# A decoder layer with 32 experts: nine named homes for the expert weights, filled in the order they come free

## The chip, the cores and the metric

The kernel runs on one core of one Trainium2 chip. The metric is the device time of one execution in microseconds (us), the median of several. Engines are named as in the profile: PE is TensorE's matmuls, PEld its weight loads, DVE is VectorE, ACT is ScalarE, POOL is GpSimd, and SP is the engine whose queue issues nearly all transfers here (the profile calls its issuing part SPq).

## The reference

One decoder layer on 256 rows of width 1024, float32. Two attention branches and an output projection come first. Then each row goes to 4 of 32 experts, and each expert has an up-projection to 2 x 1024 columns, a clamped gate, and a down-projection. The part of it that the change touches:

```
h = layer_norm(DN_ALPHA * x + mix @ w_out, ln1_g, ln1_b)
logits = h @ w_router + b_router
top_vals, top_idx = lax.top_k(logits, 4)
gates = jax.nn.softmax(top_vals)
combine = jnp.sum(jax.nn.one_hot(top_idx, 32) * gates[..., None], axis=1)
def expert(acc, p):
    wu, bu, wd, bd, c = p
    a = t @ wu + bu                                  # wu: 1024 x 2048
    g = jnp.minimum(a[:, :1024], 7.0)
    lin = jnp.clip(a[:, 1024:], -7.0, 7.0)
    y = ((lin + 1.0) * (g * jax.nn.sigmoid(1.702 * g))) @ wd + bd   # wd: 1024 x 1024
    return acc + c[:, None] * y, None
x = layer_norm(DN_ALPHA * h + ffn, ln2_g, ln2_b)
```

## The kernel before

**Two stages.** The first stage is attention and its projections. Its weights (`w_pre`) come in 1 MB tiles and are split into a high and a low part for products in three passes: ScalarE copies the high part (L149), VectorE subtracts it (L150). The pieces have names such as `wh`, `sh`, `sy`, `sacc`. This stage ends with the routing. The second stage runs the experts in 16 pairs, each expert with room for 64 rows, both experts of a pair side by side on TensorE. Rows are gathered by products with 0/1 tables (`pm`, L786), up-products are L1032, down-products L1039, and the result is scattered back to rows (L997) and added to `acc`. A check of the rows per expert (`nblk_i`) can start a loop for experts with more rows than that; with these inputs it isn't needed.

**Weights of the experts.** An expert has 8 MB of up-weights and 4 MB of down-weights. They are loaded in blocks of 2.097 MB (128 partitions x 4096 float32): `fetch_up(e, k, t)` (L961), k = 0 to 3, and `fetch_down(e, a, t)` (L965), a = 0 or 1. A pair therefore takes 12 blocks. There is room for nine blocks, 16 KB per partition each: three pools `ring4` (1), `ring3` (5) and `ringx` (3). They lie where buffers of the first stage lay, so the first block in each can be issued only when the first stage no longer reads that space. Below, the nine places are called as the changed kernel calls them: right3 is `ring4`, left0 to left4 are the five of `ring3`, right0 to right2 the three of `ringx`. `slot2()` hands them out round and round, in the order that `rings` sets:

```
rings((ring4, 1), (ring3, 3), (ringx, NX2), (ring3, NL2 - 3))
```

that is right3, left0, left1, left2, right0, right1, right2, left3, left4. The 10th block takes right3 again, and so on.

**Four halves.** For experts 0 and 1 the block k = 3 comes in halves of 1 MB, into places that are still free then: `one2`, the space of `acc` (before `acc` is used), `one1`, and `wy` in the space of `y`. They are issued by L976.

**Order.** PE, DVE and ACT issue in source order in the pair loop (`tc.manual_schedule`). SP isn't in that list: its order comes from the framework's scheduler, which may move a transfer ahead of others or behind them. SP's queue is served in order, so a transfer that waits for its space holds up all that stand behind it.

**Biases of the up-projection.** `b_up` comes in four groups of three pieces (`braw`, L575). POOL converts each to `bup` (L581, L586). `next_bup` is called before the pair loop for the first group and in the loop, at experts 2, 10 and 18, for the others.

**The last four experts** are written out behind the loop; their last down blocks come in a half (L1098) and three smaller pieces (L1103), expert by expert.

Of the kernel before, what the change touches and what calls it, by code (L numbers as in the profile page):

```python
# [10 lines left out]
F32 = mybir.dt.float32  # L11
F32R = mybir.dt.float32r
BF16 = mybir.dt.bfloat16
EN = mybir.EngineType
# [6 lines left out]
P = 128  # L21
# [3 lines left out]
KD = D // P  # L25
# [3 lines left out]
NE, TOPK, FF = 32, 4, 1024  # L29
CAP = 64  # L30
NR1, NR2, NSP = 7, 5, 3
NL2, NX2 = 5, 3
ALPHA = 2.0 ** 0.25
LN_EPS, RMS_EPS = 1e-5, 1e-6
LIMIT, SW = 7.0, 1.702
# [23 lines left out]
def decoder_layer(ctx: ExitStack, tc: tile.TileContext, A, dbg=None):  # L59
    nc = tc.nc  # L60
    te, ve, se, ge, sy = nc.tensor, nc.vector, nc.scalar, nc.gpsimd, nc.sync
# [26 lines left out]
    def slot2():  # L88

        turn[0] += 1  # L90
        return seq[(turn[0] - 1) % len(seq)].tile([P, 4096], F32, name="w2")

    def rings(*pools):
        turn[0] = 0
        seq[:] = [p for p, n in pools for _ in range(n)]
# [7 lines left out]
    src = tc.alloc_tile_pool(name="src", bufs=1)  # L103
# [36 lines left out]
    def part(w, a, k, to=None):  # L140

        if spare:
            hi, lo = spare[flip[0] % len(spare) if to is None else to]
        else:
            hi, lo = [att.tile([P, 1024], F32R, name=n, bufs=NSP) for n in ("wh", "wl")]
        n = w.shape[2]
        hi, lo = hi[:, :n], lo[:, :n]
        flip[0] += 1
        se.copy(hi, w[:, a])  # L149
        (ge if flip[0] in aside else ve).tensor_sub(lo, w[:, a], hi.bitcast(F32))  # L150
        return [t.rearrange("p (k c) -> p k c", k=k) for t in (hi, lo)]
# [396 lines left out]
    moe = ctx.enter_context(tc.tile_pool(name="moe", bufs=1, reuse_waits="tile", side="right"))  # L548
# [99 lines left out]
    for j in range(KD):  # L648
# [3 lines left out]
        w = part(wo, j % 2, KD)  # L652
# [4 lines left out]
        t = held["g", j][1]  # L657
        ve.tensor_mul(t, ps, t)
        ve.tensor_add(t[:, 0], t[:, 0], t[:, 1])
        if j:  # L660
            w = part(wu, (j - 1) % 2, 1)
# [15 lines left out]
    w = part(wu, 1, 1)  # L677
# [215 lines left out]
    acc = per.tile([P, NT, D], F32, name="acc")  # L893
# [1 line left out]
    ring1.release()  # L895
    xrows.release()
    ring2.release()
    ring3 = ctx.enter_context(tc.tile_pool(name="ring3", bufs=NL2, reuse_waits="tile"))
    one1 = ctx.enter_context(tc.tile_pool(name="one1", bufs=1, reuse_waits="tile"))
    ringx = ctx.enter_context(tc.tile_pool(name="ringx", bufs=NX2, reuse_waits="tile", side="right"))  # L900
    one2 = ctx.enter_context(tc.tile_pool(name="one2", bufs=1, reuse_waits="tile", side="right"))
    ring4 = ctx.enter_context(tc.tile_pool(name="ring4", bufs=1, reuse_waits="tile", side="right"))
    rings((ring4, 1), (ring3, 3), (ringx, NX2), (ring3, NL2 - 3))

    def add_rows(b, c, ps):
        ve.tensor_add(acc[:, b, half(c)], acc[:, b, half(c)], ps)  # L906
# [23 lines left out]
    def up_view(e):  # L930
        return A["w_up"][e].rearrange("(k p i) f -> p k (i f)", p=P, i=2)
# [25 lines left out]
    def halves_of(t):  # L957
        return t[:, :2048], t[:, 2048:]
# [5 lines left out]
    def fetch_down(e, a, t):  # L964
# [1 line left out]
        return halves_of(t)  # L966


    ahead = [(fetch_up, i, k) for k in range(KD // 2) for i in range(2)][:-2]
    ahead += [(fetch_down, i, a) for a in range(2) for i in range(2)][:NL2 + NX2 + 1 - len(ahead)]  # L970
    early = {(f, e, k): f(e, k, slot2()) for f, e, k in ahead}
    late = [[one2.tile([P, 2048], F32, name="w"), acc.rearrange("p b d -> p (b d)")],
            [one1.tile([P, 2048], F32, name="w"), moe.tile([P, 2048], F32, name="wy", tag="y")]]
    for i in range(2):
        for t, src in zip(late[i], halves_of(up_view(i)[:, KD // 2 - 1])):
            sy.dma_start(t, src)  # L976
        early[fetch_up, i, KD // 2 - 1] = late[i]

    def fetch(f, e, k):
        return early.pop((f, e, k)) if (f, e, k) in early else f(e, k, slot2())  # L980
# [7 lines left out]
    def parts_of(dn, gs):  # L988
        y = moe.tile([P, 2, FF], F32R, name="yp", tag="y")
        for c in range(2):  # L990
            parts(y, dn, gs, c)
        return y
# [33 lines left out]
    with order:  # L1026
# [18 lines left out]
        for ea in range(0, NE - 4, 2):  # L1045
# [16 lines left out]
            y = moe.tile([P, 2, FF], F32, name="y")  # L1062
# [19 lines left out]
            y = parts_of(dn, gs)  # L1082
# [34 lines left out]
        y = moe.tile([P, 2, FF], F32, name="y")  # L1117
# [39 lines left out]
        y = parts_of(dn, slots_a[1])  # L1157
# [130 lines left out]
    with tc.If(most > 1):  # L1288
        at = slot2()[:, :2048].rearrange("p (v n) -> p v n", v=4)
# [106 lines left out]
```

## Time and profile before

| what | value |
|---|---|
| median of 3 runs (lowest to highest) | 1192.05 us (1191.5 to 1192.13) |
| the profiled execution: its own time | 1190.18 us |
| its span in the profile | 1188.5 us |
| busy: PE, PEld, DVE, ACT, POOL | 93%, 47%, 28%, 19%, 11% |
| bytes moved | 439.71 MB, mean 370 GB/s over the span |
| chain that ended last, by engine | DMA 43%, PE 41%, DVE 2%, ACT 1% |

The span is what the rows below divide up. Busy shares are means over stages: the first stage moves few bytes and the second many, so the table of the profile in 40 slices and the views of single stages tell more than the means. In rows with a bracket, the number in it is the idle time just before, and behind the arrow stands what ended it.

### The profile page before, as it was taken

To read this page: it belongs to the slowest core of one execution; us is meant where nothing else is said; L and a number is where in the kernel's file an instruction comes from. 1 tells how busy PE (TensorE), PEld (TensorE's weight loads), DVE (VectorE), ACT (ScalarE), POOL (GpSimd) and SP (SyncE) were. 2 spreads that over 40 slices of the span, in tenths; PEclk is the share of its full clock that TensorE was granted. 3 is DMA by queue.
4 is the path that set the end of the run, shared out by engine and by line. 5 is a ranking of instruction groups with operands and counts; after the bars stand their busy time and mean duration, and the time that the engine had idled before them with its cause. 6 is when DMAs were issued, how large, how long until landed. Compare 5 with 4: busy or idle time off the path is not lost.

```text
span 1188.5 us, 13798 instructions
## 1 busy us (share of the span) xinstructions
PE 1109.3 (93%) x5807; PEld 554.2 (47%) x5808; DVE 332.6 (28%) x698; ACT 221.7 (19%) x427; POOL 135.9 (11%) x127
## 2 busy tenths in 40 slices
PE   8999999979999999999999999999999999999985
PEld 8987889724343443333333343333333433334322
DVE  7887637603111221111111111111111111112013
ACT  4567634311010110001010101010101010101011
POOL 6573673000000100000001000000000000000001
PEclk9999999989999999999999999999999999999998
DMA  8433752599999999999999999999999999999991
GB/s 323 178 108 142 264 189 84 228 426 427 427 427 428 426 416 427 428 426 429 425 429 426 427 428 427 426 427 427 427 428 426 428 426 427 428 426 428 427 410 69
DMA packets 37740, 439.71 MB, mean 370 GB/s; under 512 B 5621, under 2 KB 5866, under 8 KB 9386
## 3 DMA queue, kind: packets, MB, share of 16 engines
q1 hardware_dynamic: 37674, 438.79, 88.4%
q8 instruction: 47, 0.77, 0.3%
q14 instruction: 19, 0.16, 0.0%
HBM read 437.72 MB, written 1.05 MB: 369 GB/s over the span
## 4 chain that ended last, share of the span: by engine, by line
DMA 43%; PE 41%; DVE 2%; ACT 1%; issue 0%; SPq 0%; DVEq 0%; ACTq 0%
DMA w<-w_up 37%; PE bank L1039 15%; PE pair L1032 13%; DMA w<-w_down 5%; PE misc L786 4%; PE misc L926 1%; PE pair L1039 1%; ACT y L927 1%; PE misc L158 1%; PE misc L160 1%; PE misc L159 1%; PE pair L159 1%; PE pair L160 1%; PE pair L158 1%; PE misc L997 1%; DMA braw<-b_down 0%
## 5 line engine op out<-in xcount | busy, mean ns | idle before, releaser
L1032 PE MATMUL pair<-w,xg 128*64 128x512 f32 x2032 | 501.1, 599 | 41.8 <-DMA w<-w_up 41.8
L1032 PEld LDWEIGHTS pair<-w,xg 128*64 128x64 f32 x2032 | 150.3, 137 | 352.0 <-issue 272.0
L1039 PE MATMUL bank<-w,y 128*64 128x512 f32 x960 | 218.7, 596 | 5.1 <-DMA w<-w_down 3.4
L1039 PEld LDWEIGHTS bank<-w,y 128*64 128x64 f32 x960 | 73.1, 137 | 132.3 <-issue 109.2
L906 DVE TENSOR_TENSOR acc<-acc,misc 128x512 f32<-128x512 f32 x56 | 36.2, 684 | 173.5 <-PE misc L997 173.3
L158 PE MATMUL bank<-xh,wh 128*128 128x256 f32 x256 | 74.1, 290 | 4.3 <-DVE rm L211 2.5
L1009 ACT CAST pgT<-bank 128x256 fp32r<-128x256 f32 x16 | 6.0, 373 | 374.6 <-PE bank L1007 374.6
L160 PE MATMUL bank<-xh,wl 128*128 128x256 f32 x256 | 73.2, 286 | 2.0 <-DVE wl L150 2.0
L159 PE MATMUL bank<-xl,wh 128*128 128x256 f32 x256 | 72.4, 283 | 0.0
L786 PEld LDWEIGHTS misc<-pm,h 128*128 128x128 f32 x512 | 62.9, 197 | 14.2 <-issue 11.7
L786 PE MATMUL misc<-pm,h 128*128 128x128 f32 x512 | 67.4, 285 | 0.7 <-ACT y L927 0.7
L916 DVE TENSOR_SCALAR y<-pair 128x512 f32<-128x512 f32 x30 | 20.6, 688 | 166.5 <-ACT y L909 166.5
L184 POOL TENSOR_TENSOR rstd<-rstd,mhalf 128x1 f32<-128x1 f32 x4 | 2.3, 571 | 557.7 <-DVE rstd L690 557.7
L985 DVE SCALAR_TENSOR_TENSOR yp<-bank,gsl,yp 128x512 fp32r<-128x512 f32 x30 | 21.1, 747 | 157.8 <-ACT yp L984 157.8
L984 ACT ACTIVATE yp<-bank,gsl 128x512 fp32r<-128x512 f32 x30 | 19.0, 684 | 178.5 <-PE bank L1039 178.5
L158 PEld LDWEIGHTS bank<-xh,wh 128*128 128x128 f32 x256 | 48.8, 191 | 6.4 <-issue 2.6
L149 ACT CAST wh<-w 128x1024 fp32r<-128x1024 f32 (+1 forms) x42 | 42.7, 1024 | 42.6 <-PE bank L159 29.1
L160 PEld LDWEIGHTS bank<-xh,wl 128*128 128x128 f32 x256 | 48.8, 191 | 3.1 <-DVE wl L150 2.9
L159 PEld LDWEIGHTS bank<-xl,wh 128*128 128x128 f32 x256 | 48.9, 191 | 0.2 <-DVE xl L155 0.2
L774 DVE TENSOR_SCALAR xg<-misc,lnx 128x128 f32<-128x128 f32 x64 | 22.1, 404 | 92.5 <-PE misc L786 85.5
L909 ACT ACTIVATE y<-pair 128x512 f32<-128x512 f32 x30 | 17.8, 597 | 158.6 <-PE pair L1032 158.6
L581 POOL CAST bup<-braw 96x512 bf16<-96x512 f32 x4 | 2.4, 607 | 375.5 <-PE pair L800 375.4
(361 smaller groups left out, 1091.5 us busy)
## 6 DMA issues: line engine op xcount, KB each, us to landing
w<-w_up SPq DMA_DIRECT2D x126, 2048.0 KB, 32.8
w<-w_down SPq DMA_DIRECT2D x62, 2048.0 KB, 32.1
w<-w_pre SPq DMA_DIRECT2D x27, 1024.0 KB, 5.1
w<-w_up SPq DMA_DIRECT2D x2, 1024.0 KB, 17.7
w<-w_down SPq DMA_DIRECT2D x2, 1024.0 KB, 29.1
w<-w_pre SPq DMA_DIRECT2D x3, 512.0 KB, 6.7
w<-w_pre SPq DMA_DIRECT2D x2, 768.0 KB, 12.6
w<-xT SPq DMA_DIRECT2D x4, 256.0 KB, 5.7
```

The costliest lines, as they stand in the source:

```text
L149: se.copy(hi, w[:, a])
L158: te.matmul(out, lhs[0], rhs[0], start=start, stop=False)
L159: te.matmul(out, lhs[0], rhs[1], start=False, stop=False)
L160: te.matmul(out, lhs[1], rhs[0], start=False, stop=stop)
L774: ve.tensor_scalar(dst, src, lnx[:, k:k + 1], lnx[:, 8 + k:9 + k], op0=OP.mult, op1=OP.add)
L786: te.matmul(pt[:, k4], columns(b, k), pm[:, b].rearrange("p e s -> p (e s)"), start=(b == 0), stop=(b == NT - 1))
L906: ve.tensor_add(acc[:, b, half(c)], acc[:, b, half(c)], ps)
L916: ve.tensor_scalar(li, up[c][:, 1], LIMIT + 1.0, 1.0 - LIMIT, op0=OP.min, op1=OP.max)
L984: se.activation(y[:, 0, half(c)], dn[c], AF.Copy, scale=gs)
L985: ve.scalar_tensor_tensor(y[:, 1, half(c)], dn[c], gs, y[:, 0, half(c)].bitcast(F32), op0=OP.mult, op1=OP.subtract)
L1032: te.matmul(up[c % 2][64 * i:64 * i + 64, c // 2], xg[k // 4][:, k % 4, 64 * i:64 * i + 64], ws[i][:, 512 * c:512 * c + 512], start=False, ...
L1039: te.matmul(dn[c][64 * i:64 * i + 64, :], aT[:, 2 * a + j, 64 * i:64 * i + 64], ws[i][:, D * j + 512 * c:D * j + 512 * c + 512], start=Fal ...
```

## The change

The three rings become nine pools of one buffer each with names, at the same places. The order in which they are filled is set by a list. The halves of block 3 are issued between the full blocks, behind the 2nd, 6th, 7th and 8th of them (n counts from 0). And from the first expert block on SP issues in source order as well.

```diff
-    ring3 = ctx.enter_context(tc.tile_pool(name="ring3", bufs=NL2, reuse_waits="tile"))
-    one1 = ctx.enter_context(tc.tile_pool(name="one1", bufs=1, reuse_waits="tile"))
-    ringx = ctx.enter_context(tc.tile_pool(name="ringx", bufs=NX2, reuse_waits="tile", side="right"))
-    one2 = ctx.enter_context(tc.tile_pool(name="one2", bufs=1, reuse_waits="tile", side="right"))
-    ring4 = ctx.enter_context(tc.tile_pool(name="ring4", bufs=1, reuse_waits="tile", side="right"))
-    rings((ring4, 1), (ring3, 3), (ringx, NX2), (ring3, NL2 - 3))
+    def home(name, side):
+        return ctx.enter_context(tc.tile_pool(name=name, bufs=1, reuse_waits="tile", side=side))
+
+    left = [home(f"left{i}", "left") for i in range(5)]
+    one1 = home("one1", "left")
+    right = [home(f"right{i}", "right") for i in range(3)]
+    one2 = home("one2", "right")
+    right.append(home("right3", "right"))
+
+    homes = [right[3], right[1], left[1], left[2], left[0], left[3], left[4], right[2], right[0]]
+    rings(*((p, 1) for p in homes))
...
-    ahead = [(fetch_up, i, k) for k in range(KD // 2) for i in range(2)][:-2]
-    ahead += [(fetch_down, i, a) for a in range(2) for i in range(2)][:NL2 + NX2 + 1 - len(ahead)]
-    early = {(f, e, k): f(e, k, slot2()) for f, e, k in ahead}
-    late = [[one2.tile([P, 2048], F32, name="w"), acc.rearrange("p b d -> p (b d)")],
-            [one1.tile([P, 2048], F32, name="w"), moe.tile([P, 2048], F32, name="wy", tag="y")]]
-    for i in range(2):
-        for t, src in zip(late[i], halves_of(up_view(i)[:, KD // 2 - 1])):
-            sy.dma_start(t, src)
-        early[fetch_up, i, KD // 2 - 1] = late[i]
+    early = {}
+    parts_at = [[one2.tile([P, 2048], F32, name="w"), acc.rearrange("p b d -> p (b d)")],
+                [one1.tile([P, 2048], F32, name="w"), moe.tile([P, 2048], F32, name="wy", tag="y")]]
+
+    def fetch_half(e, i):
+        sy.dma_start(parts_at[e][i], halves_of(up_view(e)[:, KD // 2 - 1])[i])
+
+    in_order = ctx.enter_context(tc.manual_schedule(engines={EN.SP}))
+    for n, (f, e, k) in enumerate([(fetch_up, i, k) for k in range(KD // 2 - 1) for i in range(2)]
+                                  + [(fetch_down, 0, 0), (fetch_down, 1, 0), (fetch_down, 0, 1)]):
+        early[f, e, k] = f(e, k, slot2())
+        for at, h_e, h_i in ((1, 0, 0), (5, 0, 1), (6, 1, 0), (7, 1, 1)):
+            if n == at:
+                fetch_half(h_e, h_i)
+    for e in range(2):
+        early[fetch_up, e, KD // 2 - 1] = parts_at[e]
```

Lines of the changed kernel: L961 becomes L965, L965 becomes L969, L976 becomes L979, L575 becomes L574, L1098 and L1103 become L1110 and L1115.

**Where the stages meet, SP.** In the kernel before, from the last two tiles of the first stage (`w<-w_pre`) to the last up blocks of the first pair. Numbered names are full blocks; `w<-w_up 128x2048` and `acc` are halves.

```order
L130 DMA w<-w_pre 128x2048 x2
L961 DMA w_2703<-w_up 128x4096
L575 DMA braw<-b_up 32x512 x6
L976 DMA acc<-w_up 128x2048
L961 DMA w_2705<-w_up 128x4096
L961 DMA w_2707<-w_up 128x4096
L961 DMA w_2709<-w_up 128x4096
L965 DMA w_2717<-w_down 128x4096
L965 DMA w_2719<-w_down 128x4096
L976 DMA w<-w_up 128x2048
L961 DMA w_2711<-w_up 128x4096
L961 DMA w_2713<-w_up 128x4096
```

The first full block is followed by two groups of `b_up` and then by the half in `acc`'s space; the half in `one2` stands earlier, between tiles of the first stage. In the changed kernel the same place on SP reads:

```order
L129 DMA w<-w_pre 128x2048 x2
L965 DMA w_2726<-w_up 128x4096
L965 DMA w_2728<-w_up 128x4096
L979 DMA w<-w_up 128x2048
L965 DMA w_2731<-w_up 128x4096
L965 DMA w_2733<-w_up 128x4096
L965 DMA w_2735<-w_up 128x4096
L965 DMA w_2737<-w_up 128x4096
L979 DMA acc<-w_up 128x2048
L969 DMA w_2740<-w_down 128x4096
L979 DMA w<-w_up 128x2048
L969 DMA w_2743<-w_down 128x4096
```

Six full blocks and the half in `one2` now stand ahead of `acc`'s half, and no `b_up` group is left here.

**In the second pair, SP of the changed kernel.** The rows go from the pair's third up blocks to its first down blocks and show one of the two groups of `b_up` that stood at the place above.

```order
L965 DMA w_3046<-w_up 128x4096
L965 DMA w_3048<-w_up 128x4096
L965 DMA w_3076<-w_up 128x4096
L965 DMA w_3078<-w_up 128x4096
L574 DMA braw<-b_up 32x512 x3
L969 DMA w_3143<-w_down 128x4096
L969 DMA w_3145<-w_down 128x4096
```

The group now stands behind the pair's last up block; the next two stand at the same place of the sixth and the tenth pair. Before, only the last of these three stood among the blocks of the pair loop.

**The end, SP of the changed kernel.** The last down blocks of experts 30 and 31 (`w_5916`, `w_5918`) and the output.

```order
L1110 DMA w_5916<-w_down 128x2048
L1110 DMA w_5918<-w_down 128x2048
L1115 DMA w_5916<-w_down 128x2x512
L1115 DMA w_5918<-w_down 128x2x512
L1115 DMA w_5916<-w_down 128x512
L1115 DMA w_5918<-w_down 128x512
L1115 DMA w_5916<-w_down 128x512
L1115 DMA w_5918<-w_down 128x512
L1214 DMA out<-w_6311 128x512 x4
L1292 TENSOR_LOAD nblk_i
```

Before, all pieces of the one expert stood ahead of those of the other, and SP's read of `nblk_i` stood among the blocks of the second pair. PE, DVE and ACT have the same order as before.

## Rows read from the trace of the kernel before

**Rows 1.** The page, chain that ended last: shares of the span by line.
```profile
DMA w<-w_up 37%; PE bank L1039 15%; PE pair L1032 13%; DMA w<-w_down 5%; PE misc L786 4%; PE misc L926 1%; PE pair L1039 1%; ACT y L927 1%; PE misc L158 1%; PE misc L160 1%; PE misc L159 1%; PE pair L159 1%; PE pair L160 1%; PE pair L158 1%; PE misc L997 1%; DMA braw<-b_down 0%
```
**Rows 2.** Table by stretch: start:end us, busy (count) per engine, PE clock, DMA share, GB/s.
```profile
181.00:189.00 8.00, 8.00 (x66) 7.82 (x65) 6.08 (x9) 4.21 (x6) 0.00 (x0) 1.00 0.80 287
189.00:220.00 31.00, 31.00 (x200) 28.05 (x199) 22.99 (x27) 13.29 (x16) 10.23 (x8) 1.00 0.03 7
260.00:265.00 5.00, 2.12 (x5) 0.53 (x6) 0.00 (x0) 0.00 (x0) 0.00 (x0) 0.50 1.01 429
300.00:428.00 128.00, 127.75 (x645) 50.86 (x641) 24.43 (x48) 12.10 (x24) 4.74 (x6) 1.00 1.01 427
428.00:1080.00 652.00, 617.60 (x2844) 244.98 (x2845) 109.26 (x220) 59.91 (x122) 6.32 (x7) 1.00 1.01 427
```
**Rows 3.** Timeline of ACT, 370 to 430 us: start, duration, instruction; once per pair.
```profile
376.64 0.37 ACT L1009 CAST pgT<-bank 128x256 fp32r<-128x256 f32 x1 [19.95 <-PE bank L1007]
...
428.38 0.37 ACT L1009 CAST pgT<-bank 128x256 fp32r<-128x256 f32 x1 [19.93 <-PE bank L1007]
```
**Rows 4.** The chain in order of time, from 1100 us on: start, duration, what.
```profile
1122.41 32.55 DMA w<-w_down
...
1155.01 3.65 PE pair L1039 x14
```
**Rows 5.** Timeline of SP's queue, 180 to 221 us: start, stretch, what it issues.
```profile
180.99 0.33 SPq L961 DMA_DIRECT2D w<-w_up  x1
181.49 18.31 SPq L575 DMA_DIRECT2D braw<-b_up  x6
220.38 0.35 SPq L976 DMA_DIRECT2D acc<-w_up  x1
```
**Rows 6.** Waits of SP's queue, 181 to 221 us: total us, times, longest.
```profile
SPq L976 <- DVE sacc L150: 14.5, 1, 14.5
...
SPq L575 <- POOL bup L586: 9.0, 1, 9.0
...
SPq L976 <- PE misc L160: 6.0, 1, 6.0
```
**Rows 7.** Timeline of SP's queue, 295 to 296 us.
```profile
295.70 0.33 SPq L961 DMA_DIRECT2D w<-w_up  x1
```
**Rows 8.** DMA issues of the same instant: count, KB each, us to landing.
```profile
w<-w_up SPq DMA_DIRECT2D x1, 2048.0 KB, 9.6
```
**Rows 9.** Timeline of DVE, 165 to 215 us: splits of weights.
```profile
172.97 2.18 DVE L150 TENSOR_TENSOR sy<-w,sy 128x1024 fp32r<-128x1024 f32 x1 [7.02 <-ACT sy L149]
...
184.93 1.22 DVE L150 TENSOR_TENSOR sy<-w,sy 128x1024 fp32r<-128x1024 f32 x1
...
192.96 1.50 DVE L150 TENSOR_TENSOR sh<-w,sh 128x1024 fp32r<-128x1024 f32 x1
...
200.59 1.22 DVE L150 TENSOR_TENSOR sh<-w,sh 128x1024 fp32r<-128x1024 f32 x1
...
210.24 1.22 DVE L150 TENSOR_TENSOR sy<-w,sy 128x1024 fp32r<-128x1024 f32 x1
```
**Rows 10.** DMA issues, 180.5 to 181.4 us: count, KB each, us to landing.
```profile
w<-w_up SPq DMA_DIRECT2D x1, 2048.0 KB, 8.1
```
**Rows 11.** Timeline of PE, 234 to 304 us: products of the first pair.
```profile
236.52 7.09 PE L1032 MATMUL pair<-w,xg 128*64 128x512 f32 x32
...
245.62 7.09 PE L1032 MATMUL pair<-w,xg 128*64 128x512 f32 x32
...
263.41 5.25 PE L1032 MATMUL pair<-w,xg 128*64 128x512 f32 x14 [2.88 <-DMA w<-w_up]
...
284.03 3.65 PE L1039 MATMUL bank<-w,y 128*64 128x512 f32 x16
...
292.02 10.52 PE L1039 MATMUL bank<-w,y 128*64 128x512 f32 x48
```
**Rows 12.** Table by stretch for line L150 alone: busy (count) of DVE, then POOL.
```profile
181.00:236.50 55.50, 18.56 (x14) 0.00 (x0) 1.00 0.41 158
```

More of the change, by code (lines that the diff above doesn't have):

```diff
@@ L31 @@
 NR1, NR2, NSP = 7, 5, 3
-NL2, NX2 = 5, 3
 ALPHA = 2.0 ** 0.25
```

## The prediction

> **What bounds the kernel now.** I read the chain first: 37% of the span is waiting for up-weights to land [rows 1]. The table by stage says where [rows 2]. From 300 us to 1080 us the DMA engines are full at 427 GB/s, so a block of 2.097 MB costs 2.097/0.427 = 4.91 us, and a pair of experts (12 blocks) 58.9 us. The reader should then compare TensorE: where nothing is late, from 376.64 to 428.38, a pair takes it 51.7 us [rows 3], and in 300 to 428 us it is busy for 127.75 of 128 us [rows 2]. So TensorE catches up with the stream and then lives on it. The chain's tail shows the same: TensorE starts at 1155.01 on a down block whose transfer the chain shows from 1122.41 on, for 32.55 us, and behind it no wait on DMA stands in the chain [rows 4]. The finish is therefore the time at which the stream delivers that block, plus a tail of 33.5 us (1188.5 - 1155.0). A byte that is loaded sooner, in time that the stream has free, is worth its 1/427 GB/s at the end, unless the stream falls idle later.
>
> There is such time. From 189 to 220 us DMA moves 7 GB/s [rows 2]. SP shows why: it issues one block at 180.99, six b_up pieces from 181.49 on, and then nothing until the `acc` half at 220.38 [rows 5]. That half waited for the last users of `acc`'s space, 14.5 us and 6.0 us [rows 6]. Blocks whose space was free stood behind it in the queue.
>
> **The change, part by part.** The finish is followed through one block: the 16th full one in the queue. With the four halves, 18 blocks' worth have landed by then, in either kernel. Before, it is the transfer issued at 295.70 [rows 7], 9.6 us before its landing [rows 8]: 305.3 us. From there on the queue is fed ahead of need in both kernels.
>
> 1. Five blocks instead of one before 220 us. The first two go to right3 and right1, which are both free at 180.99. Left1 follows when the split that reads it last is through (192.96 + 1.50 = 194.5), left2 at 200.59 + 1.22 = 201.8, left0 at 210.24 + 1.22 = 211.5 [rows 9]. The distances of 7 to 10 us exceed a block's 4.91 us, and an isolated one, issued at 180.99 together with small pieces, landed after 8.1 us [rows 10], so all five are in by about 220 us. Left3 needs what `acc` needed, 220.4, and from there on the stream is full as before. The gain is 4 blocks x 4.91 = **19.6 us**. It costs TensorE nothing as long as the splits aren't slowed; that is a rival below.
>
> 2. TensorE's first pair starts at 236.52 [rows 11] in both, since it waits for routing, not for weights. Before, its third group of 16 products waited and then ran at a granted clock of 0.50, the 1.2 GHz level [rows 2]; it ended at 263.41 + 5.25 = 268.7. The 32 products ahead of it ended at 245.62 + 7.09 = 252.7, and 16 products that wait for nothing take 3.65 us [rows 11]. So 268.7 - 252.7 - 3.65 = 12.3 us go here. After the change its blocks have landed by 230 us and TensorE is 12.3 us earlier from here on. By itself this gives nothing at the end, because the stream is the bound; it decides when space comes free.
>
> 3. The stream runs dry once. Blocks 10 to 15 go into the space that the first pair's up-products leave, from the end of its first 32 products (236.52 + 7.09 = 243.6) on. But the 16th goes into left4, free when the first 16 of the 48 down-products that begin at 292.02 are over. Before, SP issued the 16th right then, 295.70, so after it is 295.7 - 12.3 = 283.4. With 19.6 us won, the 15th block would be in at 305.3 - 4.9 - 19.6 = 280.8: nothing is left to move when the 16th is issued. What a restart costs, the trace shows in a block's landing from an idle queue: 8.1 us, of which about 0.5 us are three b_up pieces (0.2 MB) [rows 10], so 7.6 us. It bounds from below at 4.9 us (no restart cost, excluded by that row) and from above at 8.1 us. The 16th lands at 283.4 + 7.6 = 291.0 instead of 285.7: **5.3 us** are given back (4.8 to 5.8). The Trainium skill's page "DMA: Bandwidth & Descriptors", section "Anatomy of one DMA - SWDGE (gpsimd) path", gives about 2.0 us fixed per transfer beside the bytes, for GpSimd's path (these blocks go by SP's). By it a lone block would take an estimated 4.9 + 2.0 = 6.9 us and 4.6 us be given back, 0.7 us less; the row shows 0.7 us more than the rule, and the sum stays with the row.
>
> 4. Two of the four b_up groups, loaded between 181.49 and 200 us before, now lie in the full stream, at the second and the sixth pair: 6 pieces of 32 x 512 float32, 64 KB each, 0.39 MB / 0.427 = **0.9 us**. POOL's conversions move with them, behind the two `rstd` steps. Their cover is TensorE, which doesn't need these biases for two more pairs at least; without the cover the nearest row is SP's wait for a conversion, 9.0 us [rows 6], once.
>
> 5. At nothing: the `one2` half moves to just behind the second block (TensorE needs it after 260 us; in 181 to 189 us the queue has room, 287 GB/s [rows 2]). The last down halves interleave: TensorE's last wait in the chain, until 1155.01, is for the block ahead of them, which keeps its place [rows 4]; a block late there would be 4.9 us. SP's read of `nblk_i` moves behind the output, whose landing the end waits for anyway.
>
> 6. The order of SP within a pair is as before. TensorE needs 51.7 us for what takes the stream 58.9, so from the second pair on space comes free ahead of the stream's turn, by up to 7.2 us more with each pair; I charge no second dry spell. One would cost a restart, 7.6 - 4.9 = 2.7 us.
>
> Sum: 19.6 - 5.3 - 0.9 = 13.4 us. The profiled execution took 1190.18 us, 1.9 us less than the median of the three runs; its forecast is 1176.8 and that of the median 1192.05 - 13.4 = **1178.7 us**. Check: the 16th block at 291.0 instead of 305.3 is 14.3 us, less 0.9.
>
> **The rivals.**
> *No dry spell.* If left4 came free before about 280 us, the whole 19.6 - 0.9 = 18.7 us would stay: 1173.4. Against it: left4 waits for down-products that can't begin before all of the pair's up-products are over, and these already run back to back in my count.
> *A longer dry spell.* Every us by which TensorE is later than 283.4 at left4 is a us at the end. For it: groups of its first pair also wait for ScalarE and VectorE (gathered rows, the spread), which I left as they were. 3 to 6 us of it would give 1181.7 to 1184.7.
> *The change doesn't do what it says.* If some early issue still waits for `acc`'s user, or for the landing of an earlier transfer, all stays at about 1192. The program's order speaks against it: the five blocks' own waits are on the splits above, and `acc` stands behind them.
> *Slower: the loads slow the splits.* Now 8.4 MB more (4 blocks) arrive while ScalarE and VectorE split the output weights. VectorE's part of one split took 2.18 us where it is usually 1.22, 0.96 us more [rows 9]. VectorE makes 14 of them from 181 us on [rows 12]. If each lost 0.96 us, ScalarE's copy ahead of each lost as much, and TensorE waited for all, 14 x 1.92 = 26.9 us would go before its first pair, and left4 come free that much later: 1178.7 + 26.9 = 1205.6. It decides from 13.4 us on, half of that. Against it: at 184.93, with DMA at 287 GB/s in 181 to 189 us, a split took 1.22 us; at 192.96, with DMA at 7 GB/s, 1.50 us [rows 2, 9].
>
> **Chances.** My forecast, 1176.5 to 1181: 0.70. No dry spell, 1173 to 1176.5: 0.08. A longer one, 1181 to 1186: 0.13. No effect: 0.05. Slower: 0.04, of which half ends within 0.2%. 0.2% is 2.4 us, about what a measurement of this kernel can tell from no change. So faster 0.91, same 0.07, slower 0.02. The range 1173.5 to 1184.5 leaves about 0.13 outside.
>
> **What would show it.** Step 1: blocks issued at about 181 (two), 194.5, 201.8, 211.5 and 220.4. Step 2: no wait of TensorE on DMA from 236 to 300 us, a granted clock of 1.00 there, the first pair's last 48 products beginning near 280 us. Step 3: a hole in DMA near 279 to 285 us and no other until 1140; the 16th block issued near 283.4. Step 4: b_up issues near 290 us and in the sixth pair. Step 5: TensorE's last wait on DMA near 1142 and a tail of 33.5 us behind it. Wrong would make it: splits above 1.3 us in 190 to 220 us, a first pair later than 236.5, a second hole, or a stream below 427 GB/s.

## The result and the profile after

The changed kernel takes 1179.62 us (median of 4 runs, 1178.41 to 1180.97) against 1192.07 us: 0.9897 of the time before, 95% interval 0.988 to 0.9914. That is 12.4 us less (10.3 to 14.3); 13.4 were forecast. On another chip the same pair gave 0.9898 (0.9883 to 0.9914). The profiled execution took 1180.39 us with a span of 1178.6 us, 9.9 us less than the span before; its own forecast was 1176.8. Of the experiment acc_second below, two of seven executions (1212.44 and 1795.98 us, the first of them the profiled one) ran at a mean granted clock of 0.85 and 0.56 instead of 0.99, so that its ratio is taken from the other five.

SP's timeline of the changed kernel around the meeting of the stages (start, stretch, what it issues), from narrow windows:

```profile
181.09 0.80 SPq L965 DMA_DIRECT2D w<-w_up  x2
194.29 0.33 SPq L965 DMA_DIRECT2D w<-w_up  x1
200.35 0.33 SPq L965 DMA_DIRECT2D w<-w_up  x1
211.58 0.33 SPq L965 DMA_DIRECT2D w<-w_up  x1
220.47 0.33 SPq L965 DMA_DIRECT2D w<-w_up  x1
220.89 0.38 SPq L979 DMA_DIRECT2D acc<-w_up  x1
...
290.58 1.31 SPq L574 DMA_DIRECT2D braw<-b_up  x3
```

Five full blocks are issued ahead of 220 us, where [rows 5] have one, and no b_up piece stands between them. The table by stretch (us, busy of PE, PEld, DVE, ACT, POOL with counts, granted clock, DMA share, GB/s) answers to [rows 2]:

```profile
181.00:189.00 8.00, 8.00 (x66) 7.83 (x65) 5.96 (x8) 4.31 (x6) 0.00 (x0) 1.00 0.89 330
189.00:220.00 31.00, 31.00 (x200) 28.04 (x199) 20.56 (x28) 13.48 (x16) 0.00 (x0) 1.00 0.75 288
260.00:265.00 5.00, 5.00 (x26) 1.70 (x24) 0.00 (x0) 0.00 (x0) 0.00 (x0) 1.00 1.02 436
275.00:280.00 5.00, 3.76 (x32) 3.13 (x32) 2.12 (x6) 0.58 (x1) 0.00 (x0) 1.00 0.77 326
280.00:285.00 5.00, 5.00 (x26) 1.72 (x24) 1.63 (x3) 0.00 (x0) 0.00 (x0) 1.00 0.23 46
285.00:290.00 5.00, 5.00 (x26) 1.59 (x24) 0.00 (x0) 0.00 (x0) 0.00 (x0) 1.00 0.92 387
300.00:428.00 128.00, 127.21 (x631) 50.14 (x627) 22.51 (x48) 11.78 (x24) 6.45 (x7) 1.00 1.01 426
428.00:1080.00 652.00, 613.50 (x2846) 243.72 (x2848) 109.08 (x220) 61.01 (x124) 12.58 (x14) 1.00 1.01 426
```

In 189 to 220 us DMA now moves 288 GB/s instead of 7. In 260 to 265 us TensorE is busy throughout at a clock of 1.00, where it stood or ran at 0.50. In 280 to 285 us there is a hole in the stream that the kernel before doesn't have: 46 GB/s. From 300 us on the stream is full again, at 426 GB/s.

TensorE's timeline, as in [rows 11], and below it its waits from 236 to 300 us (total, times, longest):

```profile
236.62 7.09 PE L1044 MATMUL pair<-w,xg 128*64 128x512 f32 x32
...
245.72 10.52 PE L1044 MATMUL pair<-w,xg 128*64 128x512 f32 x48
...
279.61 10.52 PE L1051 MATMUL bank<-w,y 128*64 128x512 f32 x48
```
```profile
PE misc L944 <- DVE xg L773: 1.2, 1, 1.2
PE misc L930 <- DVE y L922: 0.7, 1, 0.7
```

No wait on DMA is left in the first pair, and its last 48 products begin at 279.61 instead of 292.02. The first 16 of them (3.65 us) set left4 free, and SP issues the 16th block at 283.29. SP's timeline and the table of DMA issues of that instant (count, KB each, us to landing):

```profile
283.29 0.80 SPq L965 DMA_DIRECT2D w<-w_up  x2
```
```profile
w<-w_up SPq DMA_DIRECT2D x1, 2048.0 KB, 7.6
```

The timeline shows the 16th and 17th block together, the table the 16th alone. It lands at 283.29 + 7.6 = 290.9, where before it was 305.3. The end of the chain in order of time, to compare with [rows 4]:

```profile
1112.59 31.21 DMA w<-w_down
...
1143.85 5.32 PE pair L1051 x14
```

The last down block that TensorE waits for is there at 1112.59 + 31.21 = 1143.80 instead of 1154.96, 11.2 us earlier. The 14 products behind it take 5.32 us instead of 3.65. Two stretches of the table say why: the granted clock is 0.50 there, the 1.2 GHz level.

```profile
1144.00:1146.00 2.00, 2.00 (x6) 0.62 (x8) 0.00 (x0) 0.00 (x0) 0.00 (x0) 0.50 1.03 407
1146.00:1148.00 2.00, 2.00 (x8) 0.52 (x5) 0.00 (x0) 0.00 (x0) 0.00 (x0) 0.69 0.87 340
```

The tail behind the last wait is so 1178.6 - 1143.8 = 34.8 us instead of 33.5: 1.7 us more for the 14 products, some 0.4 us less in the last 10 us.

### The profile page after: what moved, and what is told of

Same layout as the page of the kernel before. It is cut to its first block, busy times and chain, and to the rows that moved or that the text cites. A ratio compares the mean times of both kernels' runs of the same rounds, so it can differ in the third digit from the quotient of the medians.

```text
span 1178.6 us, 13807 instructions
## 1 busy us (share of the span) xinstructions
PE 1104.7 (94%) x5807; PEld 551.6 (47%) x5808; DVE 329.4 (28%) x698; ACT 221.7 (19%) x427; POOL 133.7 (11%) x127
## 4 chain that ended last, share of the span: by engine, by line
PE 46%; DMA 37%; DVE 1%; ACT 1%; issue 0%; DVEq 0%; ACTq 0%
DMA w<-w_up 35%; PE bank L1051 16%; PE pair L1044 15%; PE misc L785 5%; DMA w<-w_down 3%; PE misc L930 1%; PE pair L1051 1%; ACT y L931 1%; PE misc L157 1%; PE misc L159 1%; PE misc L158 1%; PE pair L157 1%; PE pair L158 1%; PE pair L159 1%; PE bank L159 1%; PE bank L157 1%
## 5 line engine op out<-in xcount | busy, mean ns | idle before, releaser
L1051 PE MATMUL bank<-w,y 128*64 128x512 f32 x960 | 215.4, 596 | 3.4 <-DMA w<-w_down 1.6
L576 POOL TENSOR_SCALAR braw<-braw,cc 96x512 f32<-96x512 f32 x4 | 6.3, 1574 | 542.5 <-DMA braw<-b_up 542.5
```

Source lines behind the costliest of these rows:

```text
L1051: te.matmul(dn[c][64 * i:64 * i + 64, :], aT[:, 2 * a + j, 64 * i:64 * i + 64], ws[i][:, D * j + 512 * c:D * j + 512 * c + 512], start=Fal ...
```

## Experiments

The experiments put single parts of the change back, or take single costs away. The rivals were that source order on SP brings the gain, that the hole costs nothing, and that the tail's order matters. Three groups were measured, each on one chip with the kernel before beside it: acc_second, sp_free, sp_only and tenth_home (kernel before 1190.97 us); after_again, no_bup, tail_apart and both (1190.92); halves_last, one_piece and both_one (1190.90). Ratios are to the kernel before of the same group, and kernels of different groups are compared by their ratios.

**acc_second.** The half in `acc`'s space goes back in front of all full blocks but the first (the half in `one2`, which has room there, moves one place forward with it):

```diff
-        for at, h_e, h_i in ((1, 0, 0), (5, 0, 1), (6, 1, 0), (7, 1, 1)):
+        for at, h_e, h_i in ((0, 0, 0), (0, 0, 1), (6, 1, 0), (7, 1, 1)):
```

> The changed kernel with one thing put back: the half in acc's space stands second among the expert loads, as before, so that SP waits there until about 220 us; the new fill order, the interleaved halves and SP's source order stay. Theory (the gain is the four blocks loaded before 220 us): nothing is gained, and the b_up groups in the stream cost 0.9 us by their bytes or up to 4 us by the landings seen: 1193 to 1196 us. Rival (the gain comes from source order on SP or the new fill order later on): 1185 us or less.

Measured: 1195.7 us, 1.0035 of the kernel before (1.0022 to 1.0048). In its profile SP issues one full block ahead of `acc`'s half and five right behind it. With `acc`'s half in front, the whole gain is gone, though the new fill order and SP's source order are still there. The gain is made while SP would wait for that half. What is left is a loss of 4 us; the two b_up groups in the stream are some 2.9 us of it (step 4 below), and no run shows what the rest is.

**sp_free.** SP's order goes back to the scheduler:

```diff
-    in_order = ctx.enter_context(tc.manual_schedule(engines={EN.SP}))
```

> The changed kernel without source order on SP: the scheduler orders it, with nine homes and the new fill order. It puts six b_up pieces behind the first block, then left1, left2, left0, right1 ahead of acc's half. Theory: five blocks are still in by about 224 us, the 16th is still issued when left4 comes free, near 283 us, and two b_up groups are out of the stream: 1175.5 to 1179 us, the same as the changed kernel or 1 to 4 us faster. Rival (source order on SP is needed for the gain): 1185 us or more.

Measured: 1176.24 us, 0.9879 (0.9865 to 0.9894), as expected. Source order on SP isn't needed for the gain. From its SP timeline:

```profile
180.58 0.33 SPq L965 DMA_DIRECT2D w<-w_up  x1
...
199.36 0.37 SPq L965 DMA_DIRECT2D w<-w_up  x1
201.31 0.35 SPq L965 DMA_DIRECT2D w<-w_up  x1
211.07 1.72 SPq L965 DMA_DIRECT2D w<-w_up  x2
...
282.78 0.33 SPq L965 DMA_DIRECT2D w<-w_up  x1
```

Five blocks are again issued before 220 us, though three of the five places (right1, left1, left2) are filled later than in the changed kernel, and the 16th again waits for left4, at 282.78. As the dry spell sets when the 16th block lands, being late by a few us earlier costs nothing. The last awaited down block is in at 1109.52 + 31.19 = 1140.7 (its chain), 3.1 us ahead of the changed kernel. Of these, 0.5 us were there from the first block on (180.58 against 181.09), and some 2.6 are left for the two b_up groups that this kernel has less in its stream.

```profile
1109.52 31.19 DMA w<-w_down
```

**sp_only.** The kernel before with SP's source order alone:

```diff
+    in_order = ctx.enter_context(tc.manual_schedule(engines={EN.SP}))
     early = {(f, e, k): f(e, k, slot2()) for f, e, k in ahead}
```

> The kernel before with source order on SP from the first expert block on, and nothing else: old pools, old fill order, halves behind the nine blocks. Left0 is second and free at 211.5 us only. Theory: the stream is full from about 213.5 instead of 222.4 us (8.9 us), less a half that was loaded early (2.5 us), less b_up (0.9 to 4 us): 1186.5 to 1189.5 us, no dry spell. Rival (SP's order alone brings the gain): about 1180 us; rival (it brings nothing): 1192 us.

Measured: 1194.46 us, 1.0031 (1.0019 to 1.0042). Slower than before, and 5 to 8 us above the expectation. The error is in the third place of the old fill order, for which left1 was expected. SP's timeline:

```profile
211.65 0.33 SPq L961 DMA_DIRECT2D w<-w_up  x1
...
222.67 0.33 SPq L961 DMA_DIRECT2D w<-w_up  x1
```

The third block waits until 222.67, which is when left4 is free, not left1 (194.29 in the changed kernel). The addresses in the built program agree: the pool of five hands out its places as left0, left4, left3, left2, left1, and the pool of three as right2, right0, right1. The order of the nine given in the section on the kernel before is thus wrong in names; the prediction's sum goes by the changed kernel's own order and by waits, so the error doesn't touch it. Source order with the old fill order wins one block ahead of 222 us, but moves `one2`'s half behind nine blocks. Its waits on TensorE from 236 to 300 us and its table show the price, the clock among it:

```profile
PE pair L1033 <- DMA w<-w_up: 6.5, 2, 3.5
```
```profile
265.00:270.00 5.00, 1.51 (x4) 0.54 (x6) 0.00 (x0) 0.00 (x0) 0.00 (x0) 0.50 1.04 434
```

TensorE again waits for up-weights in its first pair. The 16th block was issued at 294.35 and landed 10.9 us later, at 305.2, as before the change, and three b_up groups lie in the stream.

**halves_last.** The changed kernel with its halves behind the nine blocks:

```diff
-        for at, h_e, h_i in ((1, 0, 0), (5, 0, 1), (6, 1, 0), (7, 1, 1)):
-            if n == at:
-                fetch_half(h_e, h_i)
+        if n == 8:
+            for at in ((0, 0), (0, 1), (1, 0), (1, 1)):
+                fetch_half(*at)
```

> The changed kernel with the four 1 MB halves behind all nine blocks, as the kernel before has them in its source, instead of between them; fill order and SP's source order stay. Theory (the fill order alone brings the early blocks; the halves land by about 253 us, TensorE needs them at 260): the same as the changed kernel, 0.9898 of the kernel before, no wait of TensorE in its first pair. Rival (the interleaving matters): the halves land behind 260 us, TensorE waits there and the gain shrinks by 2 us or more.

Measured: 1178.67 us, 0.9901 (0.9886 to 0.9916), the same as the changed kernel, and TensorE doesn't wait for up-weights in its first pair. So the interleaving isn't needed as long as SP issues in source order, and sp_free shows that source order isn't needed as long as the halves are interleaved. What the kernels with the gain share is the new fill order with `acc`'s half behind the early blocks; sp_only shows that source order without that fill order brings nothing, acc_second that the fill order without that place of `acc`'s half brings nothing. The fill order with neither source order nor interleaving wasn't run.

**tenth_home.** The 16th block goes elsewhere:

```diff
     def fetch(f, e, k):
+        if (f, e, k) == (fetch_up, 3, 2):
+            ts = [p.tile([P, 2048], F32, name="w") for p in (one2, one1)]
+            for t, src in zip(ts, halves_of(up_view(e)[:, k])):
+                sy.dma_start(t, src)
+            return ts
         return early.pop((f, e, k)) if (f, e, k) in early else f(e, k, slot2())
```

> The changed kernel, but the 16th block goes in two halves into the space of one2 and one1, which the first pair's up-products leave at about 264 us, instead of into left4 at 283 us; the 17th goes to left4, and so on round. Theory (the dry spell near 281 to 286 us costs 5.3 us): no hole in DMA there, 1174.3 us, 1173 to 1175.5. Rival (the time is lost elsewhere anyway, or a second hole follows): 1178 us or more.

Measured: 1175.11 us, 0.9863 (0.9849 to 0.9877), 4 us less than the changed kernel by the ratios. SP issues the two halves at 263.86, and the hole is closed:

```profile
263.86 0.80 SPq L995 DMA_DIRECT2D w<-w_up  x2
```
```profile
280.00:285.00 5.00, 5.00 (x26) 1.64 (x24) 1.45 (x3) 0.00 (x0) 0.00 (x0) 1.00 1.00 370
```

370 GB/s instead of 46. Its last awaited down block is in at 1107.31 + 31.38 = 1138.7 by the chain, 5.1 us ahead of the changed kernel:

```profile
1107.31 31.38 DMA w<-w_down
```

The dry spell was a cost, and of the size in the sum (5.3; 0.2 of the 5.1 us were there from the first block on, 180.91 against 181.09). By the ratios it is nearer 4, with intervals of some 1.7 us to either side of each.

**no_bup.** The three b_up groups of the loop are left out, with their conversions on POOL; experts 8 to 31 then compute with the biases of the first eight:

```diff
-                next_bup(ea // 8 + 1)
+                bup[ea // 8 + 1] = bup[0]
```

> The changed kernel without the three b_up groups of the pair loop (experts 8 to 31 get the biases of the first eight), so without their 9 pieces of 64 KB and their conversions. Theory, by the landings of the changed kernel and by the difference to the kernel that loads two groups early (2.7 us for two): 3.5 to 5 us faster than the changed kernel. Rival (they cost their bytes, 0.45 us a group): 1.4 us faster.

Measured: 1176.61 us, 0.988 (0.9863 to 0.9897), 2 us less than the changed kernel on the same chip, between the two expectations. The profiles tell more than the times: the last awaited down block is in at 1108.07 + 31.22 = 1139.3, against 1112.19 + 31.19 = 1143.4 for the changed kernel of the same chip (after_again), 4.1 us for three groups. The two profiles of the changed kernel agree here within 0.4 us. The chains, no_bup first:

```profile
1108.07 31.22 DMA w<-w_down
```
```profile
1112.19 31.19 DMA w<-w_down
```

Of the tables of the changed kernel and then of this one, the stretch in which the second group lands:

```profile
530.00:545.00 15.00, 13.13 (x60) 4.55 (x60) 0.31 (x2) 0.37 (x1) 3.33 (x3) 1.00 1.01 400
```
```profile
530.00:545.00 15.00, 13.98 (x64) 4.65 (x60) 0.31 (x2) 0.78 (x2) 0.00 (x0) 1.00 1.01 429
```

The DMA engines are busy all the time in both (1.01), but move 400 instead of 429 GB/s. Over 15 us that is 15 x 29 / 427 = 1.0 us, and with the 0.46 us for the group's own bytes about 1.5 us a group. In 770 to 785 us, where the third group lands, it is 392 instead of 427, about 1.7 us.

**one_piece.** Each group comes as one piece, and POOL copies it to the other two places:

```diff
-        for i in range(3):
+        for i in range(1 if name == "up" else 3):
             sy.dma_start(raw[32 * i:32 * i + 32], rows[32 * g:32 * g + 32])
         if name == "up":
+            for i in (1, 2):
+                ge.tensor_copy(raw[32 * i:32 * i + 32], raw[:32])
```

> The changed kernel with one 64 KB piece for each b_up group instead of three with the same contents; POOL copies it to the other two places. Theory (each piece in the full stream costs some 0.45 us, three times its bytes' time): the six pieces saved give 2 to 3 us against the changed kernel. Rival (a group costs the stream about 1.4 us however many pieces it has): no change. Rival (only the bytes count): 0.9 us.

Measured: 1177.11 us, 0.988 (0.9865 to 0.9896). The last awaited down block is in at 1109.91 + 31.20 = 1141.1, 2.3 to 2.7 us ahead of the two profiles of the changed kernel (1143.4 and 1143.8):

```profile
1109.91 31.20 DMA w<-w_down
```

That is some 0.4 us for each of the six pieces saved, against 0.15 us for their bytes, so the rivals of a fixed price per group and of a price by bytes alone are out by the profiles. The ratios give 2.1 us, with intervals of some 1.8 us to either side, and tell none of this apart. The table shows the rest of the price, in the same stretch as above:

```profile
530.00:545.00 15.00, 13.58 (x62) 4.65 (x60) 0.31 (x2) 0.37 (x1) 4.79 (x6) 1.00 1.00 413
```

A group of one piece still costs 15 x 16 / 427 + 0.15 = 0.7 us, about half of a group of three. POOL works longer here than in the changed kernel (4.79 against 3.33 us) and the stream loses less, so POOL's work isn't what slows it. Whether it is the number of pieces or their size that sets the price stays open, as both went down together.

**tail_apart.** The last down pieces expert by expert, as before:

```diff
         for e in (eb, eb + 1):
             wdn[e, 1] = halves_of(slot2())
+        for e in (eb, eb + 1):
             sy.dma_start(wdn[e, 1][0], halves_of(down_view(e)[:, 1])[0])
-        for c, js in ((0, slice(0, 2)), (1, slice(0, 1)), (1, slice(1, 2))):
-            for e in (eb, eb + 1):
+            for c, js in ((0, slice(0, 2)), (1, slice(0, 1)), (1, slice(1, 2))):
```

> The changed kernel with the last down halves and pieces issued expert by expert, as before, instead of interleaved. Theory (the last wait is for the block ahead of them): the same as the changed kernel within 0.7 us. Rival (the interleaving delays the first of the last products, or brings the half clock at 1144 us): 1.7 us or more faster.

Measured: 1180.55 us, 0.9909 (0.9896 to 0.9923): not faster. It is 1.5 us slower than the changed kernel, more than the 0.7 us expected but within the intervals. Its 14 products behind the last wait took 5.27 us, so the half clock there doesn't come from the interleaving.

**after_again.** The changed kernel, unedited.

> The changed kernel itself, on the chip of the next three. Theory: 0.9897 of the kernel before, 1178 to 1181 us, with single runs some 2.5 us apart: one run had TensorE at a granted clock of 0.50 where its last products begin (1144 us), which costs 1.7 us, and other runs need not have it.

Measured: 1179.01 us (1178.5 to 1180.55), 0.9898 (0.9883 to 0.9914). This profile too had the half clock behind the last wait (5.34 us).

**both** and **both_one.** The edit of tenth_home with that of sp_free, and then with that of one_piece as well.

> Two edits together: the 16th block in the space of one2 and one1, and no source order on SP, so that two b_up groups are loaded before 200 us. Theory (the two costs add): 5.1 us for the dry spell and 2.7 us for b_up, 7 to 8.5 us faster than the changed kernel, no hole near 281 us, 0.9820 to 0.9835 of the kernel before. Rival (one hides the other, since the early b_up groups push back left1): no faster than the tenth-home kernel, 0.9863.

Measured: 1172.96 us, 0.985 (0.9832 to 0.9869), 6 us less than the changed kernel; tenth_home and sp_free alone gave 4 and 2. It is short of the 7 to 8.5 us expected, and its interval reaches the rival's 0.9863. By the profile most of both savings is there: the last awaited down block is in at 1105.41 + 31.61 = 1137.0, 6.8 us ahead of the changed kernel with the same start (181.09), where the parts were 4.9 and 2.6.

```profile
1105.41 31.61 DMA w<-w_down
```

There is no hole:

```profile
280.00:285.00 5.00, 5.00 (x26) 1.72 (x24) 1.64 (x3) 0.00 (x0) 0.00 (x0) 1.00 1.04 416
```

> The kernel with the 16th block in the space of one2 and one1 and without source order on SP, and with one b_up piece a group as well. Only one group is left in its stream. Theory: 0.9 us faster than without the last edit, 0.984 to 0.985 of the kernel before. Rival (POOL's two copies make SP wait longer between the two early b_up groups, and left1 is issued later): the same or slower.

Measured: 1170.71 us, 0.9834 (0.9818 to 0.985), the fastest of all, 20.2 us less than the kernel before. Its difference to both is within the intervals. In its profile TensorE began its first pair 1.5 us earlier than in both (235.11 against 236.63), and the last awaited down block came 1.5 us earlier too (1135.5 against 1137.0): the profile shows no gain of the last edit beside that earlier start.

## Why the prediction was right

*The bound.* Right: the last wait of the chain is again for a down block. One reading of it was loose. The 37% of [rows 1] are transfers on the chain; TensorE itself, busy for 93% of the span, worked through most of them. Its waits on up-weights from 230 us on, in the kernel before, add up to 41.8 us in 46 times:

```profile
PE pair L1032 <- DMA w<-w_up: 41.8, 46, 5.9
```

*Step 1, four blocks early.* Right, issue by issue: 181 (two), 194.5, 201.8, 211.5 and 220.4 were forecast; 181.1, 194.3, 200.4, 211.6 and 220.5 were seen. acc_second shows that without it nothing of the gain is left. The splits weren't slowed: the table by stretch for VectorE's line of them (L149 now) has 17.11 us for the 14, against 18.56 [rows 12], and TensorE's first pair begins at 236.62 instead of 236.52.

```profile
181.00:236.50 55.50, 17.11 (x14) 0.00 (x0) 1.00 0.82 318
```

*Step 2, TensorE 12.3 us earlier.* Right: 292.02 - 279.61 = 12.4.

*Step 3, the dry spell.* Right in place, cause and size: the 16th block was forecast to be issued at 283.4 and to land at 291.0, and was at 283.29 and 290.9. The restart takes 7.6 us, as was worked out from [rows 10]. The rule of the Trainium skill's page "DMA: Bandwidth & Descriptors", section "Anatomy of one DMA - SWDGE (gpsimd) path", 2.0 us beside the bytes, gives an estimate of 6.9 us, 0.7 us short here too. The rival without a dry spell would have been a kernel with a place for the 16th block, and tenth_home is that kernel: 1175.11 on a chip where the kernel before took 1190.97.

*Step 4, b_up.* The term that was mis-sized. 0.9 us were charged for the bytes of two groups. A group costs 1.4 to 1.5 us (4.1 us for three in no_bup, 1.5 by the throughput at the second), so two cost some 2.9 us; sp_free, without two, is some 2.6 us earlier at the last down block. What failed is the pricing by bytes: one_piece saved some 0.4 us a piece, where the bytes are 0.15.

*Step 5, at nothing.* The tail's order cost nothing (tail_apart), nor did the place of `one2`'s half (halves_last). What the step didn't have is the half clock at 1144 us: 5.32 - 3.65 = 1.7 us in this profile, so the tail wasn't the 33.5 us forecast.

*Step 6, no second dry spell.* Right: 426 GB/s from 300 us on. The prediction named a stream below 427 as a sign of being wrong. The 1 GB/s is worth 780 / 427 = 1.8 us by these rounded figures, which fits b_up (step 4); from 300 to 1140 us no stretch of 10 us falls below 377 GB/s.

The sum over the profiles is then: 14.4 us at the 16th block, as forecast; of these 11.2 are left at the last down block, since b_up takes 2.9 (0.9 were charged) and 0.3 us stay unexplained; the tail takes 1.3 us more (34.8 against 33.5), which leaves 9.9. So the profiled execution is 3.6 us above its forecast of 1176.8: 2.0 by b_up, 1.3 by the tail, 0.3 unexplained. The medians differ by 12.4 us (11.9 in the group of after_again) and the median is only 0.9 us above its forecast, because the profiled execution of the kernel before was 1.9 us below its median and that of the changed kernel 0.8 above. That the forecast of the median came so near is in part luck.

What stays open is why the clock is halved behind the last wait in some kernels. It was in the two profiles of the changed kernel (the one above and after_again) and in those of tail_apart, tenth_home, one_piece and both_one, and not in those of the kernel before, sp_free, sp_only, no_bup, halves_last and both. Ahead of it TensorE waits 2.3 us in the changed kernel as in the kernel before, and in the 4 us ahead of its restart it was busy for 1.69 and 1.68 us. No edit was found that decides it. Both profiles of the changed kernel had it, so whether executions of one kernel differ in it isn't shown either.

## What to carry to other kernels

Where a kernel lives on a weight stream, look for the stretch in which the stream is idle and ask what stands at the head of its queue: here one half-block whose space came free at 220 us stood ahead of four blocks whose places came free by 212 us. The order of the queue must then be the order in which the places come free; moving the half alone won one block of the four (sp_only). Follow one later block through the change, with the event that frees its space and the time at which the stream would reach it: the later of the two counts, and that gave the dry spell and its price. Price small transfers in a full stream from a row in which some landed, and not by their bytes.

## What the runs showed of the hardware

A group of three pieces of 64 KB in a full stream cost it about 1.5 us, three times the 0.46 us of its bytes, while the DMA engines show no idle time (a share of 1.01 at 400 instead of 429 GB/s). A group of one such piece cost about 0.7 us.

A 2 MB block that was issued when the stream had run dry landed after 7.6 us, and after 7.7 us in after_again; 4.9 us of it are its bytes at 427 GB/s.

TensorE's granted clock fell to 0.50 for some 3 us behind a wait of 2.1 to 2.3 us in six of twelve profiles and not in the others, with the same 14 products behind the wait.
